# A hybrid four-branch mixer layer on one core: early merge-gate pairs, a first mLSTM chunk beside the last pairs, and block sums made operand by operand

## The chip, the core and the metric

The program runs on one core of one Trainium2 chip. Its time is device microseconds of one execution. Tile (a list scheduler with its own estimates of durations) turns the program text into one fixed instruction order per engine; priorities given in the text and the pools of tiles decide that order.

## What is computed

`x` is 2048 tokens by 1024 channels, float32. One layer, cut to what matters (in full it works chunkwise where that is said):

```python
def reference(x, norm_g, w_in, ..., w_branch, w_out, final_g):
    h = rmsnorm(x, norm_g)
    u = h @ w_in                               # 1024 -> 10256 columns
    (lru_x, lru_z, m_x, m_o, m_z, h_q, h_f, h_i, h_z,
     g_q, g_k, g_v, g_lr, g_z, merge) = split(u)
    y_a = rg_lru(causal_conv(lru_x)) * silu(lru_z)
    xm = silu(causal_conv(m_x))
    hm = sigmoid(m_o) * mlstm_chunkwise(q(xm), k(xm), v(m_x), log_i, log_f)
    y_b = (head_layernorm(hm) + m_skip * xm) * silu(m_z)
    y_c = head_rmsnorm(hgrn2(h_q, h_f, h_i)) * silu(h_z)
    y_d = head_rmsnorm(gla(g_q, g_k, g_v, g_lr)) * silu(g_z)
    proj = einsum('bsnw,nwd->bsnd', stack([y_a, y_b, y_c, y_d]), w_branch)
    merged = sum(sigmoid(merge) * proj, axis=2)
    return rmsnorm(x + merged @ w_out, final_g)
```

Every product is made to float32 accuracy from operands split in two parts: a high part (a copy rounded by ScalarE) and a low part (the difference), and three matmuls: high by high, high by low, low by high.

## The kernel before, in words

The tokens go through in two halves of 1024. In each half the stages follow one another in the program text, while the scheduler lets neighbours overlap.

*Input and first gates.* `load_first` (in half 0) loads and normalises the first 512 tokens and makes five merge gates from them; the result of each is taken from its bank by VectorE (line 353). Line 680 applies the norm to the other 512 tokens. `split_first` (line 305 ScalarE, line 306 VectorE or GpSimd) makes the operands a11 and a12 of the first tokens; x11, x12, x21, x22 are the four blocks of two token blocks by two channel blocks, four tiles each.

*Block sums.* `split_blocks` makes the other operands: a22 as it is, and the sums s1 to s4 (lines 375 to 378), each split again by lines 305 and 306. It goes tile by tile (k = 0 to 3), all operands of a tile before the next tile. The low parts of s1 and s2 are made by GpSimd, the rest by VectorE. The block x21 is kept in DRAM for later.

*Pairs.* `ahead_pairs` computes 33 pairs of column tiles per half. `ip_pair` computes one pair in Winograd's form: seven products of 12 matmuls (line 422, 128x512) with sums of weights (line 427) and of results (line 431) on VectorE; line 437 is ScalarE's copy of the first product out of its bank; the weight of each product is split by ScalarE (line 416) and GpSimd (line 417). Weights are loaded into three tiles `wr` and two tiles `gth`. The order of the pairs is a table, `GORD`: ('g', n) is n pairs of merge gates, ('z', n) n pairs of the paths that mixers use (mx, mo, mz, hq, hz, gz, gq, gk in this order), ('r', n) n pairs for the RG-LRU, ('d', n) the HGRN decays of number n, 'm' a step of the mLSTM's rows, and 't' sets an activation table. A gate pair leaves VectorE little after the sums. A pair of mx leaves a causal convolution (line 706, VectorE) and its silu (line 763). A pair of the RG-LRU has that convolution, the recurrence's gates (line 735, 24 matmuls of TensorE in the stretches counted below) and a scan. Results go to DRAM by SP's queue.

*Mixers.* `restore_block` loads x21 again. `mixers` interleaves the mLSTM's chunks (a generator `mlstm()`, eight chunks of 128 tokens a half, four heads each; `LEAD` = 8 of its steps are issued first) with tiles of HGRN2 and GLA and with merge-gate tiles that keep TensorE busy. In a chunk, lines 836 and 844 load xm and rows, line 855 computes the scores, lines 864, 871 and 880 values and transposes, line 892 and behind it transposes of the output gate and the rest. Line 227 (Ln) and line 1084 (Exp) are the root of a head's norm.

*Merge and output.* The branches' products and gates (line 268; the last gates' tanh, line 1301), then the output projection (line 280) and the final norm; rows leave by line 1358.

*Memory.* `Arena` holds NU = 16 units of 128 x 516 floats; pairs take their two result tiles from its first NG = 10 units and temporary tiles from the others. The first pairs' units for s1, s2 and s4 belong to tiles that in half 1 lie over the output rows of half 0.

In the trace's names, `wh`, `wl`, `hh`, `hl` and `s` are high and low parts (`s` of the sums), `mx` and `pb` are the eight banks that collect matmuls, `arena` is any unit, `ma` and `mb` tiles over the operands' places. `<-` stands between what is written and what is read.

Of the kernel before, what the change touches and what calls it, by code (L numbers as in the profile page):

```python
# [17 lines left out]
HT = 1024  # tokens of a half  # L18
DM = 1024
KT = 8  # k tiles of d_model  # L20
U = 516  # columns of one arena unit
NU = 16  # arena units that stay
NA = 4  # tiles of two units that are the arena's outside of the fast products
NY = 8  # the same, and branch outputs in the merge
NP = 6  # merge gates (of 32) computed between the mixers
NE = 5  # of these, so many for the first tokens while the others are split
EPS = 1e-6
NPB = 2  # PSUM banks of the input projection; the other ones are the mixers'
NG = 10  # arena units of the fast products; the other ones are what follows them
PRE = (("mx", 4), ("mo", 4), ("mz", 4), ("hq", 4), ("hz", 4), ("gz", 4), ("gq", 2), ("gk", 2))  # paths to DRAM, with their tiles  # L30
# [5 lines left out]
NW = 6  # L36
DG = (0,1)
# [4 lines left out]
GORD = [('r',1),('z',2),('r',1),('z',2),('r',1),('z',2),('r',1),('z',6),('g',8),('t',0),('m',0),('g',1),('m',0),('g',1),('m',0),('g',1),('m',0),('d',0),('m',0),('g',99),('d',1),('z',2)]  # L42
NORM = {"hz": "hnw", "gz": "gnw"}  # gate paths with the norm's weight in them
SILU = ("lz", "mz", "hq", "hz", "gz")
FILL = [0, 2, 0, 0, 0, 1, 0, 0, 1, 0, 0, 0, 2, 0]  # merge gates projected before each stage of the mixers

# columns of the packed per-channel vectors
# [10 lines left out]
# channel-major column tiles of the input projection, in the order of wc  # L58
# [10 lines left out]
# constants that depend on shapes alone  # L69
# [29 lines left out]
class Arena:  # L99
    """Units of U columns, handed out in program order, round and round; pairs start at even units."""  # L100
# [47 lines left out]
class Trunk:  # L148
    def __init__(self, ctx, tc, a, out, dbg=None):
# [8 lines left out]
        self.wr = [c.tile([P, 528], F32, name=f"wr{k}") for k in range(3)]  # L158
# [9 lines left out]
        self.mi = 0  # L168
        self.ydram = [self.dram.tile([4, P, HT], F32, name=f"y{n}") for n in range(4)]
# [34 lines left out]
    def bank(self):  # L204
        self.mi += 1
        return self.mx[self.mi % (8 - NPB)]

# [31 lines left out]
    def wpieces(self, aps):  # L239
        nc = self.nc  # L240
        r = []
        with self.prio(self.EV):
            for ap in aps:
                w = ap.shape[-1]
                i = self.wi
                self.wi += 1
                raw, hi, lo = self.wr[i % 3][:, :w], self.wh[i % NW][:, :w], self.wl[i % NW][:, :w]
                nc.sync.dma_start(raw, ap)
                nc.scalar.activation(hi, raw, AF.Copy)  # L249
                nc.gpsimd.tensor_tensor(lo, raw, hi, op=ALU.subtract)  # L250
                r.append((hi, lo))
# [4 lines left out]
    def proj_ch(self, pieces, rh, rl, sink, ns=(0, 1)):  # L256
        """128 columns of a product for 512 tokens at a time from weight pieces of 4 k tiles
        each: sink(token slice, PSUM [128, 512])."""
# [23 lines left out]
    def ip_tok(self, pieces, ncol, evac, single=8):  # L282
        """Token-major column group: evac(first chunk, PSUM [128 tokens, chunks, ncol]); chunks one by one from some."""
# [10 lines left out]
    def ip_tok_k(self, pieces, evac, ks):  # L294
        """The same for 256 columns, k outermost: the operands' tiles are done with one by one."""
# [13 lines left out]
    def split_first(self, xs):  # L309
        """The normalised input of the first tokens"""  # L310
# [7 lines left out]
    def load_first(self, xs):  # L318
        """The first tokens, and merge gates from them before the norm's factor is known"""
# [40 lines left out]
    def split_blocks(self, xs, st):  # L360
        """The other blocks (two of tokens by two of channels) that the products take: one more as it
        is, four sums; the block left out goes to DRAM."""
        nc = self.nc
        V, G = nc.vector, nc.gpsimd
        a, b = slice(0, 512), slice(512, 1024)

        def own(name, i, k):
# [3 lines left out]
        for k in range(4):  # L371
            x11, x21, x12, x22 = xs[k][:, a], xs[k][:, b], xs[4 + k][:, a], xs[4 + k][:, b]
            self.split("a22", self.hh[4 + k][:, b], self.hl[4 + k][:, b], x22, V)
            nc.sync.dma_start(self.adram[k], x21)
            V.tensor_tensor(x22, x21, x22, op=ALU.add)
            V.tensor_tensor(x21, x11, x21, op=ALU.subtract)
            V.tensor_tensor(x11, x22, x11, op=ALU.subtract)
            V.tensor_tensor(x12, x12, x11, op=ALU.subtract)
            self.split("s2", *own("s2", 0, k), x11, G)
            self.split("s3", self.hh[k][:, b], self.hl[k][:, b], x21, V)  # L380
            self.split("s1", *own("s1", 1, k), x22, G)
            self.split("s4", *own("s4", 2, k), x12, V)
        self.free(*xs)

    def restore_block(self):
        """The block left out of the products, where its sum was."""
# [13 lines left out]
    def ip_pair(self, t0, t1, fin):  # L400
# [57 lines left out]
    def ahead_pairs(self):  # L458
# [10 lines left out]
        def temp():  # L469
            return self.T(NG, NU)  # L470

# [1069 lines left out]
```

## Time and profile before

| | us |
|---|---|
| three runs | 2739.0, 2732.94, 2736.58 |
| median | 2736.58 |
| profiled execution, span | 2737.5 |
| TensorE busy | 2603.8 (95%) |
| GpSimd busy | 1499.7 (55%) |
| VectorE busy | 1736.1 (63%) |
| ScalarE busy | 1291.6 (47%) |

The profiled execution shows no time of its own beside its span, so the span is taken for it. Half 0's pairs run from about 52 to 760 us, its mixers to about 1200, its merge and output to about 1420; half 1 follows in the same order. The busy time of TensorE counts a matmul from its issue to a modelled end, with waits inside, so a stretch in which matmuls stand further apart can still look busy; how many matmuls a stretch holds says more.

### The profile page before, as it was taken

What the parts mean: (1) busy time and instruction counts of PE and PEld (TensorE: products, weight loads), DVE (VectorE), ACT (ScalarE), POOL (GpSimd) and SP (SyncE); (2) the same over time, 40 slices, a digit from 0 to 9 for tenths busy, and PEclk for the clock granted to TensorE, in tenths of its full rate; (3) what the DMA queues carried; (4) which work ended last, traced back from release to release, by engine and by line L of the source; (5) the groups of instructions that cost most, each with busy time, mean ns of one, the idle gap of its engine ahead of it and who ended that gap; (6) DMA issues with size and microseconds to landing.
All of it is one profiled execution on the core that took longest, in us unless ns stands there. A gap on an engine that the chain in (4) does not pass through costs nothing. (4 is left out here: it accounts for less than half of the span.)

```text
span 2737.5 us, 45829 instructions
## 1 busy us (share of the span) xinstructions
PE 2603.8 (95%) x16800; PEld 2153.6 (79%) x16800; DVE 1736.1 (63%) x2907; ACT 1291.6 (47%) x2763; POOL 1499.7 (55%) x1273
## 2 busy tenths in 40 slices
PE   7889999999989898999999999999999999999999
PEld 5667788877878876778977777888787888777789
DVE  8987853346667767743478878533477677776332
ACT  5554554334444565542465545533344445644433
POOL 5556644444546545567476666444455556554753
PEclk9999999999999999999999999999999999989999
DMA  6132334243454435795442322433335533458821
GB/s 227 61 109 89 101 119 139 98 145 103 148 170 128 121 121 189 253 317 165 155 138 94 110 91 89 139 116 108 135 113 179 167 118 106 146 190 308 273 93 74
DMA packets 227072, 393.03 MB, mean 144 GB/s; under 512 B 20720, under 2 KB 78080, under 8 KB 226848
## 3 DMA queue, kind: packets, MB, share of 16 engines
q1 hardware_dynamic: 226848, 390.11, 42.7%
q8 instruction: 132, 2.16, 0.3%
q14 instruction: 92, 0.75, 0.1%
HBM read 270.42 MB, written 119.60 MB: 142 GB/s over the span
## 5 line engine op out<-in xcount | busy, mean ns | idle before, releaser
L417 POOL TENSOR_TENSOR wl<-wr,wh 128x512 fp32r<-128x512 f32 x264 | 371.6, 1411 | 302.4 <-ACT wh L416 294.4
L417 POOL TENSOR_TENSOR wl<-gth,wh 128x512 fp32r<-128x512 f32 x198 | 284.4, 1437 | 294.6 <-ACT wh L416 284.2
L422 PE MATMUL mx<-s,wh 128*128 128x512 f32 x1296 | 408.5, 395 | 11.3 <-DVE s L306 4.7
L431 DVE TENSOR_TENSOR arena<-arena,mx 128x512 f32<-128x512 f32 x348 | 229.4, 681 | 221.8 <-PE mx L422 208.5
L250 POOL TENSOR_TENSOR wl<-wr,wh 128x512 fp32r<-128x512 f32 (+1 forms) x176 | 250.4, 1431 | 175.4 <-ACT wh L249 139.8
L422 PE MATMUL mx<-hh,wh 128*128 128x512 f32 x760 | 302.0, 397 | 11.9 <-DVE arena L431 10.2
L422 PE MATMUL mx<-hh,wl 128*128 128x512 f32 x760 | 302.3, 398 | 3.1 <-POOL wl L417 3.1
L422 PE MATMUL mx<-hl,wh 128*128 128x512 f32 x760 | 302.0, 397 | 2.0 <-DVE hl L306 2.0
L422 PEld LDWEIGHTS mx<-s,wh 128*128 128x128 f32 x1296 | 243.9, 188 | 70.6 <-DVE s L306 7.1
L268 PE MATMUL pb<-hh,wh 128*128 128x512 f32 x704 | 286.9, 409 | 7.4 <-ACT hh L1284 2.6
L268 PE MATMUL pb<-hl,wh 128*128 128x512 f32 x704 | 286.5, 407 | 5.8 <-DVE hl L1285 5.8
L268 PE MATMUL pb<-hh,wl 128*128 128x512 f32 x704 | 284.3, 404 | 0.0
L416 ACT ACTIVATE wh<-wr 128x512 fp32r<-128x512 f32 x264 | 164.5, 627 | 232.7 <-PE mx L422 98.4
L280 PE MATMUL pb<-wh,hh 128*128 128x256 f32 (+1 forms) x880 | 254.2, 290 | 3.7 <-ACT arena L1006 1.5
L422 PE MATMUL mx<-s,wl 128*128 128x512 f32 x648 | 256.2, 396 | 0.9 <-POOL wl L417 0.9
L280 PE MATMUL pb<-wl,hh 128*128 128x256 f32 (+1 forms) x880 | 253.4, 288 | 1.7 <-POOL wl L250 1.7
L280 PE MATMUL pb<-wh,hl 128*128 128x256 f32 (+1 forms) x880 | 253.5, 288 | 0.0
L416 ACT ACTIVATE wh<-gth 128x512 fp32r<-128x512 f32 x198 | 124.4, 629 | 246.6 <-DVE gth L427 201.6
L249 ACT ACTIVATE wh<-wr 128x512 fp32r<-128x512 f32 (+1 forms) x176 | 110.0, 629 | 161.9 <-PE pb L268 106.6
L422 PEld LDWEIGHTS mx<-hh,wh 128*128 128x128 f32 x760 | 144.3, 190 | 50.1 <-ACT arena L218 11.0
L422 PEld LDWEIGHTS mx<-hh,wl 128*128 128x128 f32 x760 | 143.6, 189 | 41.0 <-POOL wl L417 8.2
L422 PEld LDWEIGHTS mx<-hl,wh 128*128 128x128 f32 x760 | 144.0, 189 | 38.1 <-DVE hl L306 3.2
(614 smaller groups left out, 6177.6 us busy)
## 6 DMA issues: line engine op xcount, KB each, us to landing
wr<-in_wc_dram SPq DMA_DIRECT2D x246, 256.0 KB, 2.7
g<-arena SPq DMA_DIRECT2D x52, 512.0 KB, 3.4
gth<-in_wc_dram SPq DMA_DIRECT2D x66, 256.0 KB, 2.8
wr<-in_wb_dram SPq DMA_DIRECT2D x64, 256.0 KB, 3.0
hl<-y SPq DMA_DIRECT2D x32, 512.0 KB, 5.9
arena<-g SPq DMA_DIRECT2D x48, 256.0 KB, 3.9
arena<-in_xT_dram SPq DMA_DIRECT2D x32, 256.0 KB, 5.1
lw<-g SPq DMA_DIRECT2D x32, 256.0 KB, 3.4
```

Source lines behind the costliest of these rows:

```text
L249: nc.scalar.activation(hi, raw, AF.Copy)
L250: nc.gpsimd.tensor_tensor(lo, raw, hi, op=ALU.subtract)
L268: nc.tensor.matmul(ps, w[:, ws], h[:, ts], start=(k == 0 and i == 0), stop=(k == nk - 1 and i == 2))
L280: self.nc.tensor.matmul(v, h[:, cs], w[:, ws], start=(first and i == 0), stop=(last and i == 2))
L416: A.activation(hi, w, AF.Copy)
L417: G.tensor_tensor(lo, w, hi, op=ALU.subtract)
L422: nc.tensor.matmul(ps, wp[:, ws], xp, start=(k == 0 and i == 0), stop=(k == 3 and i == 2))
L431: V.tensor_tensor(o, x, y, op=ALU.add)
```

## The change

- `NU` grows from 16 to 22 units, `NV` = 16 keeps the pairs' temporary tiles to units 10 to 15. The memory comes from a smaller scratch of the kernel's dynamic DMA (`dynamic_dma_scratch_size=1024`). A fourth raw weight tile is added for the gate and output projections (`NR` = 4; the pairs still use three).
- `split_blocks` works operand by operand: s2 for all four tiles, then s1, s4, s3, a22; four more units hold the sum s2.
- In the first pair of a half the product with a12 comes second and waits in its bank until it is added.
- `GORD` starts with two gate pairs, and gate pairs stand between those of the RG-LRU and of mx.
- 'c' in `GORD` is one step of `mlstm()`: the loads and scores of the first chunk are issued before the last two path pairs, in units 16 to 21. The mixers then issue two steps less at their start.

```diff
-NU = 16
+NU = 22
+NV = 16
+NR = 4
-GORD = [('r',1),('z',2),('r',1),('z',2),('r',1),('z',2),('r',1),('z',6),('g',8),('t',0),('m',0),('g',1),('m',0),('g',1),('m',0),('g',1),('m',0),('d',0),('m',0),('g',99),('d',1),('z',2)]
+GORD = [('g',2),('r',1),('z',1),('g',1),('z',1),('r',1),('g',1),('z',2),('r',1),('g',1),('z',2),('r',1),('z',6),('g',3),('t',0),('m',0),('g',1),('m',0),('g',1),('m',0),('g',1),('m',0),('d',0),('m',0),('g',99),('d',1),('c',0),('z',1),('c',0),('z',1)]
...
     def bank(self):
+        if self.pairs:
+            return self.bank8()
...
-        for k in range(4):
-            x11, x21, x12, x22 = xs[k][:, a], xs[k][:, b], xs[4 + k][:, a], xs[4 + k][:, b]
-            self.split("a22", self.hh[4 + k][:, b], self.hl[4 + k][:, b], x22, V)
-            nc.sync.dma_start(self.adram[k], x21)
-            V.tensor_tensor(x22, x21, x22, op=ALU.add)
-            V.tensor_tensor(x21, x11, x21, op=ALU.subtract)
-            V.tensor_tensor(x11, x22, x11, op=ALU.subtract)
-            V.tensor_tensor(x12, x12, x11, op=ALU.subtract)
-            self.split("s2", *own("s2", 0, k), x11, G)
-            self.split("s3", self.hh[k][:, b], self.hl[k][:, b], x21, V)
-            self.split("s1", *own("s1", 1, k), x22, G)
-            self.split("s4", *own("s4", 2, k), x12, V)
+        ds = [self.T(0, NU) for k in K]
+        for k in K:
+            d = ds[k][:, :512]
+            nc.sync.dma_start(self.adram[k], x21[k])
+            V.tensor_tensor(x11[k], x11[k], x21[k], op=ALU.subtract)
+            V.tensor_tensor(d, x22[k], x11[k], op=ALU.subtract)
+            self.split("s2", *own(0, k), d, G)
+        for k in K:
+            V.tensor_tensor(x21[k], x21[k], x22[k], op=ALU.add)
+            self.split("s1", *own(1, k), x21[k], G)
+        for k in K:
+            V.tensor_tensor(x12[k], x12[k], ds[k][:, :512], op=ALU.subtract)
+            self.split("s4", *own(2, k), x12[k], V)
+        for k in K:
+            self.split("s3", self.hh[k][:, b], self.hl[k][:, b], x11[k], V)
+        for k in K:
+            self.split("a22", self.hh[4 + k][:, b], self.hl[4 + k][:, b], x22[k], V)
+        self.free(*ds)
...
-    def ip_pair(self, t0, t1, fin):
+    def ip_pair(self, t0, t1, fin, first=False):
...
         p = product("a11", b11)
         with self.prio(self.EV):
             A.activation(c11, p, AF.Copy)
+        if first:
+            q = product("a12", b21)
         wsum(b11, b12, b11)
         wsum(w2, b22, b11)
         p = product("s2", w2)
         add(c21, c11, p)
+        if first:
+            add(c11, c11, q)
...
-        p = product("a12", b21)
-        add(c11, c11, p)
+        if not first:
+            p = product("a12", b21)
+            add(c11, c11, p)
...
+            elif n == "c":
+                self.ar.base, self.ar.lim = NV, NU
+                with self.prio(RLAT):
+                    next(self.other)
+                self.ar.base, self.ar.lim = 0, None
...
-            for _ in range(LEAD):
+            for _ in range(LEAD - 2):
                 next(other, None)
...
-    nc = bacc.Bacc("TRN2", target_bir_lowering=False, num_devices=1)
+    nc = bacc.Bacc("TRN2", target_bir_lowering=False, num_devices=1, dynamic_dma_scratch_size=1024)
```

Line numbers of the changed file are larger: 306 becomes 311, 353 becomes 358, 375 and 376 (the sums of x22 with x21, and of x11 with x21) become 387 and 383, 417 becomes 432, 427 becomes 442, 227, 1084 and 1301 become 232, 1114 and 1331.

**VectorE, at the start of half 0's pairs.** Before, around the first block sums (`gth_95<-pb_98` is the fifth gate's result, the `mqk`, `gx` and `gv` copies belong to the setup):

```order
L680 SCALAR_TENSOR_TENSOR arena<-arena,pvt,xb_247 128x512 x8
L427 TENSOR_TENSOR wr_79<-wr_80,wr_79 128x512
L306 TENSOR_TENSOR hl_75<-arena,hh_67 128x512
L306 TENSOR_TENSOR hl_76<-arena,hh_68 128x512
L353 TENSOR_TENSOR gth_95<-pb_98,xa_235 128x512
...
L375 TENSOR_TENSOR arena<-arena 128x512 x3
L427 TENSOR_TENSOR gth_95<-wr_81,wr_79 128x512
L375 TENSOR_TENSOR arena<-arena 128x512
```

Now:

```order
L383 TENSOR_TENSOR arena<-arena 128x512 x4
L311 TENSOR_TENSOR hl_75<-arena,hh_67 128x512
L311 TENSOR_TENSOR hl_76<-arena,hh_68 128x512
L358 TENSOR_TENSOR gth_96<-pb_99,xa_236 128x512
...
L384 TENSOR_TENSOR arena<-arena 128x512 x4
L387 TENSOR_TENSOR arena<-arena 128x512 x4
L311 TENSOR_TENSOR hl_71<-arena,hh_63 128x512
L311 TENSOR_TENSOR hl_72<-arena,hh_64 128x512
L311 TENSOR_TENSOR hl_73<-arena,hh_65 128x512
L311 TENSOR_TENSOR hl_74<-arena,hh_66 128x512
L311 TENSOR_TENSOR hl_78<-arena,hh_70 128x512
```

The differences of x11 and x21 (L383) moved ahead of the fifth gate's result, and the last low part of a12 (`hl_78`) behind the sums of s2 and s1 and the low parts of s3.

**GpSimd, at the start of half 1's pairs.** Before:

```order
L417 TENSOR_TENSOR wl_93<-wr_79,wh_87 128x512
L417 TENSOR_TENSOR wl_90<-wr_81,wh_84 128x512
L417 TENSOR_TENSOR wl_89<-wr_79,wh_83 128x512
L417 TENSOR_TENSOR wl_91<-wr_80,wh_85 128x512
L306 TENSOR_TENSOR s_0_11366<-arena,s_0_11366 128x512
L306 TENSOR_TENSOR s_4_11370<-arena,s_4_11370 128x512
L306 TENSOR_TENSOR s_1_11367<-arena,s_1_11367 128x512
```

Now:

```order
L311 TENSOR_TENSOR s_0_11367<-arena,s_0_11367 128x512
L311 TENSOR_TENSOR s_1_11368<-arena,s_1_11368 128x512
...
L311 TENSOR_TENSOR s_6_11373<-arena,s_6_11373 128x512
L311 TENSOR_TENSOR s_7_11374<-arena,s_7_11374 128x512
L432 TENSOR_TENSOR wl_94<-wr_79,wh_88 128x512
L432 TENSOR_TENSOR wl_92<-wr_81,wh_86 128x512
L432 TENSOR_TENSOR wl_89<-gth_95,wh_83 128x512
```

The weights' low parts (`wl`) of the first pair stood ahead of the eight low parts of s1 and s2 and now stand behind them.

**ScalarE, near the end of half 0's mixers** (ACT_TABLE_LOAD brings in the tables of the function that follows). Before, the two loads behind the tanh of the gates:

```order
L1082 ACTIVATE arena,ssq_205<-mx_99 128x128 x4
L227 ACT_TABLE_LOAD
L227 ACTIVATE ssq_204<-ssq_204,small 128x4
L227 ACTIVATE ssq_205<-ssq_205,small 128x4
L1084 ACT_TABLE_LOAD
L1084 ACTIVATE ssq_204<-ssq_204 128x4
```

Now, from the first tanh on:

```order
L1331 ACT_TABLE_LOAD
L1331 ACTIVATE arena<-arena 128x512
L1112 ACTIVATE arena,ssq_205<-mx_105 128x128 x4
L232 ACT_TABLE_LOAD
L232 ACTIVATE ssq_205<-ssq_205,small 128x4
L1112 ACTIVATE arena,ssq_206<-mx_100 128x128
L1114 ACT_TABLE_LOAD
L1114 ACTIVATE ssq_205<-ssq_205 128x4
L1112 ACTIVATE arena,ssq_206<-mx_100 128x128 x3
L1120 ACTIVATE arena<-mx_105,ssq_205 128x128 x4
L232 ACT_TABLE_LOAD
L232 ACTIVATE ssq_206<-ssq_206,small 128x4
```

Four more head norms stand behind the first tanh than before, and loads between them; the whole program has 49 loads where it had 29.

## Rows read from the trace of the kernel before

**Rows 1.** The page, part 1: busy time, share of the span, instructions.

```profile
PE 2603.8 (95%) x16800; PEld 2153.6 (79%) x16800; DVE 1736.1 (63%) x2907; ACT 1291.6 (47%) x2763; POOL 1499.7 (55%) x1273
```

**Rows 2.** Windows: start:end, length; busy us (instructions) of PE, PEld, DVE, ACT, POOL; clock, DMA.

```profile
50.00:100.00 50.00, 35.95 (x136) 25.64 (x136) 49.46 (x76) 21.79 (x35) 30.76 (x20) 0.93 0.11 32
100.00:150.00 50.00, 46.41 (x187) 36.38 (x186) 45.92 (x57) 27.15 (x43) 31.91 (x21) 0.93 0.36 125
...
200.00:250.00 50.00, 49.60 (x215) 39.84 (x214) 30.87 (x40) 23.45 (x38) 28.37 (x23) 1.00 0.28 90
```

**Rows 3.** Windows of line 422 alone: TensorE's matmuls, its weight loads.

```profile
50.00:86.00 36.00, 23.66 (x84) 15.91 (x84) 0.95 0.12 37
86.00:200.00 114.00, 93.97 (x373) 73.46 (x373) 0.94 0.26 88
400.00:550.00 150.00, 150.00 (x649) 121.68 (x648) 1.00 0.35 116
1422.00:1440.00 18.00, 14.15 (x58) 10.59 (x59) 1.00 0.36 126
1440.00:1550.00 110.00, 91.60 (x373) 71.97 (x372) 0.95 0.24 82
```

**Rows 4.** Windows of line 735 alone, the RG-LRU's gate matmuls.

```profile
50.00:200.00 150.00, 6.96 (x24) 4.19 (x24) 0.94 0.23 76
1400.00:1550.00 150.00, 6.39 (x24) 4.35 (x24) 0.97 0.32 111
```

**Rows 5.** Timeline of TensorE: start, us, instruction [idle before <- what ended it].

```profile
63.77 0.69 PE L422 MATMUL mx<-s,wh 128*128 128x512 f32 x2 [3.45 <-DVE gv L625]
...
164.47 0.77 PE L422 MATMUL mx<-hh,wh 128*128 128x512 f32 x1 [5.09 <-DVE arena L431]
```

**Rows 6.** Timeline of VectorE in half 0's first pairs.

```profile
55.58 2.83 DVE L375 TENSOR_TENSOR arena<-arena 128x512 f32<-128x512 f32 x3
...
60.05 1.75 DVE L375 TENSOR_TENSOR arena<-arena 128x512 f32<-128x512 f32 x1
...
149.34 5.59 DVE L706 SCALAR_TENSOR_TENSOR arena<-arena,hmc 128x512 f32<-128x512 f32 x6
...
162.45 1.88 DVE L431 TENSOR_TENSOR arena<-arena,mx 128x512 f32<-128x512 f32 x3
```

**Rows 7.** Timeline of GpSimd in half 0, the first splits of sums.

```profile
57.95 4.97 POOL L306 TENSOR_TENSOR s<-arena,s 128x512 fp32r<-128x512 f32 x3 [1.29 <-ACT s L305]
```

**Rows 8.** Timelines of GpSimd and of ScalarE at the start of half 1's pairs.

```profile
1424.12 12.47 POOL L306 TENSOR_TENSOR s<-arena,s 128x512 fp32r<-128x512 f32 x8
...
1422.25 6.35 ACT L305 ACTIVATE s<-arena 128x512 fp32r<-128x512 f32 x12
```

**Rows 9.** Timeline of TensorE at the mixers' start, half 0 and half 1.

```profile
763.94 1.09 PE L880 MATMUL mx<-cst,ma 128*128 128x128 f32 x4 [6.48 <-DMA ma<-pxm]
...
788.90 1.40 PE L855 MATMUL mx<-ma,mqk 128*128 128x128 f32 x5 [3.66 <-DVE mmu L922]
...
2117.72 1.65 PE L855 MATMUL mx<-ma,mqk 128*128 128x128 f32 x6 [3.81 <-DMA ma<-pxm]
```

**Rows 10.** Line 836, a chunk's load: landing; then who waited, us, times.

```profile
DMA to landing us min/median/max: 2.7/3.1/8.1
...
  PE mx L855: 12.8, 9
```

**Rows 11.** Windows of the mixers, half 0 and half 1, as in rows 2.

```profile
756.00:1200.00 444.00, 405.15 (x4206) 346.96 (x4205) 306.04 (x678) 222.17 (x645) 228.73 (x240) 0.95 0.54 175
2112.00:2560.00 448.00, 418.84 (x4275) 359.89 (x4274) 311.27 (x684) 228.01 (x659) 240.44 (x249) 0.95 0.55 181
```

**Rows 12.** Timeline of ScalarE around a table load, and the window it lies in.

```profile
1196.83 1.28 ACT L227 ACT_TABLE_LOAD   x1
1198.12 0.48 ACT L227 ACTIVATE ssq<-ssq,small 128x4 f32<-128x4 f32 x2
...
1180.00:1200.00 20.00, 20.00 (x119) 15.52 (x118) 4.80 (x10) 10.10 (x29) 5.25 (x5) 1.00 0.91 307
```

More of the change, by code (lines that the diff above doesn't have):

```diff
@@ L157, in __init__ @@
         self.hl = [c.tile([P, HT], F32R, name=f"hl{k}") for k in range(KT)]
-        self.wr = [c.tile([P, 528], F32, name=f"wr{k}") for k in range(3)]
+        self.wr = [c.tile([P, 528], F32, name=f"wr{k}") for k in range(NR)]
         self.wh = [c.tile([P, 528], F32R, name=f"wh{k}") for k in range(NW)]
@@ L168, in __init__ @@
         self.mi = 0
+        self.pairs = False
         self.ydram = [self.dram.tile([4, P, HT], F32, name=f"y{n}") for n in range(4)]
@@ L246, in wpieces @@
                 self.wi += 1
-                raw, hi, lo = self.wr[i % 3][:, :w], self.wh[i % NW][:, :w], self.wl[i % NW][:, :w]
+                raw, hi, lo = self.wr[i % NR][:, :w], self.wh[i % NW][:, :w], self.wl[i % NW][:, :w]
                 nc.sync.dma_start(raw, ap)
@@ L365, in split_blocks, with own @@
         a, b = slice(0, 512), slice(512, 1024)
-        def own(name, i, k):
+        K = range(4)
+        def own(i, k):
             t = st[4 * i + k]
             return t[:, 0:512], t[:, U:U + 512]
-        for k in range(4):
-            x11, x21, x12, x22 = xs[k][:, a], xs[k][:, b], xs[4 + k][:, a], xs[4 + k][:, b]
-            self.split("a22", self.hh[4 + k][:, b], self.hl[4 + k][:, b], x22, V)
-            nc.sync.dma_start(self.adram[k], x21)
-            V.tensor_tensor(x22, x21, x22, op=ALU.add)
-            V.tensor_tensor(x21, x11, x21, op=ALU.subtract)
-            V.tensor_tensor(x11, x22, x11, op=ALU.subtract)
-            V.tensor_tensor(x12, x12, x11, op=ALU.subtract)
-            self.split("s2", *own("s2", 0, k), x11, G)
-            self.split("s3", self.hh[k][:, b], self.hl[k][:, b], x21, V)
-            self.split("s1", *own("s1", 1, k), x22, G)
-            self.split("s4", *own("s4", 2, k), x12, V)
+        x11, x21 = [xs[k][:, a] for k in K], [xs[k][:, b] for k in K]
+        x12, x22 = [xs[4 + k][:, a] for k in K], [xs[4 + k][:, b] for k in K]
+        ds = [self.T(0, NU) for k in K]
[16 more added lines that the diff above has]
+        self.free(*ds)
         self.free(*xs)
@@ L405, in ip_pair @@
         with self.prio(self.EV):
-            b11, b12, b22 = (r[:, :512] for r in self.wr)
+            b11, b12, b22 = (r[:, :512] for r in self.wr[:3])
             b21, w2 = self.gth
@@ L469, in temp @@
         def temp():
-            return self.T(NG, NU)
+            return self.T(NG, NV)
         def silu2(n, x):
@@ L531, in ahead_pairs @@
         rows = (i for h in range(2) for i in self.mlstm_rows(h, temp))
+        self.other = self.mlstm()
+        self.pairs = True
+        first = True
         for n, i in GORD:
@@ L537, in ahead_pairs @@
                     next(rows, None)
-            if n in "tm":
+            elif n == "c":
[3 more added lines that the diff above has]
+                self.ar.base, self.ar.lim = 0, None
+            if n in "tmc":
                 continue
             for tiles, fin in ({"g": g, "z": z, "r": r}[n][:i] if n != "d" else [decays([2 * i, 2 * i + 1])]):
-                self.ip_pair(*tiles, fin)
+                self.ip_pair(*tiles, fin, first)
+                first = False
             if n != "d":
@@ L544, in ahead_pairs @@
         assert not g and not z and not r and next(rows, 1)
+        self.pairs = False
     def setup(self):
@@ L1185, in mixers @@
         self.gates_ahead(next(fill))
-        other = self.mlstm()
+        other = self.other
         due = 0.0
```

## The prediction

> **What bounds the kernel.** The engine table comes first: TensorE is busy for 95% of the span [rows 1], so time can only be won where its matmuls stand apart. The windows of the first pairs show such a place. From 50 to 150 us TensorE is busy for 35.95 and 46.41 of each 50 us, VectorE for 49.46 and 45.92. From 200 to 250 us VectorE falls to 30.87 and TensorE rises to 49.60 [rows 2]. VectorE limits the early pairs, and nothing after them.
>
> Waiting matmuls count as busy, so I count matmuls instead. From 400 to 550 us nothing waits: 649 of line 422 in 150 us, 0.2311 us each [rows 3]; a product of 12 takes 2.77 us, a pair of 84 takes 19.4. Half 0 from 50 to 86 us has 84 of them [rows 3], worth 19.4 of 36 us. From 86 to 200 us there are 373, and 24 of the RG-LRU's own [rows 3, 4]: 397 x 0.2311 = 91.7 of 114 us, so 22.3 lost. Half 1, whose pairs begin at about 1422 us, has 58 by 1440 [rows 3], worth 13.4 of 18; then 373 and 24 by 1550 [rows 3, 4], worth 91.7 of 110, so 18.3 lost. (A few records may be missing from a trace, which makes these losses upper bounds.)
>
> The timelines tell why. TensorE waits 3.45 us at 63.77 for operands, and 5.09 us at 164.47 for an addition of line 431 [rows 5]. Before that addition VectorE ran convolutions of line 706, six in 5.59 us from 149.34 on; the three additions came at 162.45, behind more of them [rows 6]. An addition sets a bank free, so TensorE stops when several additions stand behind convolutions.
>
> **The change part by part. Order of the pairs.** A pair costs VectorE eleven sums of 1.88/3 = 0.63 us [rows 6], 7 us, whatever its kind; a gate pair has little more. A pair of mx adds twelve taps of 5.59/6 = 0.93 us [rows 6] and four more operations, by the same rates 22 in all; a pair of r adds six taps, eight operations and two scans, at the tap's rate 22 too. TensorE takes 19.4. Before, r, mx, mx, r stand first: 4 x 2.6, over 10 us of backlog, on top of the splits' own. Now it is g, g, r, mx, g, mx, r, g: a gate pair gives over 10 us back ahead of every second debtor, so 2 x 2.6, some 5 us, are owed at most. The two output tiles and the banks let TensorE run a product or two, 3 to 6 us, ahead. So I keep 5 of the 22.3 us in half 0, **17.3 won**, and 4 of the 18.3 in half 1, **14.3 won**. Bounds: nothing, if a backlog of 5 us still stops the banks; all of both.
>
> **Operand by operand, half 0.** The differences of x11 and x21 now stand ahead of the fifth gate's result (the block of VectorE's rows shown): four of 2.83/3 = 0.94 us [rows 6], so the first pair starts some 3.5 us later than before. Then a11 and most of a12 run, 22 matmuls; the last split of a12 (hl_78) stands behind eight sums and four splits. Beside GpSimd's splits one operation of VectorE took 1.75 us at 60.05, without them 0.94 [rows 6, 7]. The block of eight is 8 x 4.97/3 = 13.3 us of GpSimd [rows 7]. With eight of VectorE's thirteen operations at 1.75 and five at 0.63, from 57 on, hl_78 is ready at 74; with all at 0.94, at 69. From then on little waits: by 86 us 22 + 12/0.2311 = 74 matmuls, or 95, against 84. I take 78, since three operations of 1.75 stand in the row for three splits: **1.4 lost**, between 2.3 lost and 2.5 won. With the order: 16, between 2 lost and 25.
>
> **Operand by operand, half 1.** On GpSimd the eight splits now stand ahead of the first pair's weights; before, four weights came first. They take 12.47 us, ScalarE's twelve copies 6.35 from 1422.25 on [rows 8], and cannot start sooner, since four of the tiles lie where the last output rows leave. So TensorE has no weight before 1428.6 and starts near 1430, at first at the lower clock: some 35 matmuls by 1440 against 58 [rows 3], 23 x 0.2311 = **5.3 lost**. With the 14.3 this is 9 won, between 0 and 16.
>
> **First chunk beside the last pairs.** The chunk's scores move about 229 matmuls ahead of the pairs' end, into 22 - 16 = 6 units of their own. Its matmuls and its work on ScalarE and VectorE are not less; late pairs leave VectorE free [rows 2]. Its loads join SP's queue behind writes of the same data; each holds the queue for a landing, 3.1 us by the median [rows 10], while the next pair's weights are asked for four products, 11 us, ahead. With that cover gone, each would cost 3. What vanishes: TensorE's waits at the mixers' start, 6.48 and 3.66 us in half 0, 3.81 in half 1 [rows 9], 13.95 in all. Late next is the first chunk's output gate (the transposes of line 892 come first there in the changed order), whose load waits for the last pair's units and lands, 3.1 [rows 10], then the second chunk's, an estimate of 1.4 more: 9 for two halves. **5 won**, between 0 and 9.
>
> **Head norms among tanh.** With one chunk less behind the border, the merge's first tanh (line 1301) stands ahead of six head norms per half instead of two. Ln, Exp and Tanh alternate, and ScalarE loads a table 49 times where it did 29 times, all twenty more at the two ends of the mixers. One takes 1.28 us [rows 12]: 25.7 us of ScalarE. Before, such loads fell into 20 us in which TensorE was busy throughout and ScalarE half the time [rows 12]. That nearest row says nothing lost; as TensorE's order is fixed and each load holds a head's result, I charge **3 us**, between 0 and 25.7.
>
> In the row no idle time stands around a load: it ends at 1198.11, the next instruction begins at 1198.12 [rows 12]. The Trainium skill (ScalarE: Activation LUTs, What ACT_TABLE_LOAD costs) adds a drain of 1380 ns to each of 1283 ns, 2.66 us per switch, and its section on table sets wants calls batched by set, which speaks against this change. By that page twenty switches hold ScalarE for 53 us instead of 25.7. The row disagrees on the drain, and I go by the row.
>
> **The rest.** The first product keeps its bank of eight until a12 is added: nothing, or one product, 2.8, if banks run short. A fourth raw weight buffer and the wider arena let loads start sooner in the mixers, where TensorE idles for 444 - 405.15 = 39 and 448 - 418.84 = 29 us [rows 11]; I take nothing, between 14 lost and 14 won. The smaller scratch serves no queue used here.
>
> **The sum.** 2737.5 - 16 - 9 - 5 + 3 = 2710.5. The profiled execution is 0.9 us above the median of the runs, 2736.58, so the time is **2710**.
>
> **Rivals.** *More than that:* arena and fourth buffer also take a third of the mixers' 68 us of idle time [rows 11], 23 less: 2687. For it: the mixers wait for loads [rows 9, 10]. Against: most units were there already.
>
> *The loss only moves:* VectorE's work is the same, so the convolutions meet later pairs. Then the order's 31.6 are not won: about 2741 (2737.5 + 1.4 + 5.3 - 5 + 3 - 0.9). For it: VectorE has 5 of 100 us to spare [rows 2]. Against: from 200 us on it has 19 of 50 [rows 2].
>
> *The first pairs wait longer:* blocks of splits on two engines that hinder each other delay TensorE by another 4 us in half 0 and 6 in half 1: 2720. For it: the 1.75 us [rows 6]. Against: the operands were made in one go before as well.
>
> *Tables on the path:* every load delays TensorE by its 1.28 us [rows 12]; 22.7 more than charged, 2732. For it: heads at the end of a half have few others beside them. Against: merge products fill TensorE there [rows 12]. (With the page's 2.66 us it would be 2760.)
>
> *Slower:* the mLSTM's chunk loads are issued sooner into the wider arena, among the other mixers' on one queue, and land later. TensorE already waits for them, 12.8 us over nine waits; the longest landing is 8.1 against 3.1 [rows 10]. If each of sixteen chunks is later by 3 us of those 5, that is 48: 2758. It decides from 27/16 = 1.7 us per chunk on. Against: a chunk less behind the border leaves more time per load.
>
> **Chances.** As forecast 0.58, more 0.13, longer first pairs 0.08, the loss moves 0.10, tables 0.06, slower 0.05. A measurement of this kernel tells 0.2%, 5.5 us, from no change. The first three are faster by more than that, and parts of the next two: 0.84. Of those two 0.10 is no change and 0.01 slower, with the last case 0.06. The range reaches down past the second case to 2682, and up to 2731, past longer first pairs and nearly to the tables.
>
> **What would show it.** Right: 440 or more of the pairs' matmuls from 86 to 200 us and no wait over 3 us for an addition there; TensorE idle for some 8 us after 1422; waits of 4 to 5 us at the border, the transposes' first; table loads at the mixers' ends without gaps of TensorE behind them. Wrong: pairs after 200 us that lose what the early ones win, gaps of over 1 us behind table loads, or idle time in the mixers above 39 and 29 us.

## The result, and the profile after

The changed kernel takes 2800.8 us (median of 4 runs, 2799.45 to 2809.91) against 2737.79 for the one before (4 runs, 2732.94 to 2743.06): a ratio of 1.0243, 95% interval 1.0221 to 1.0265. It is 63 us slower where 27 us faster was forecast. The rest of this text takes the 63 us apart.

The page's first parts, of the kernel after:

```profile
span 2799.9 us, 45661 instructions
...
PE 2628.1 (94%) x16800; PEld 2174.8 (78%) x16800; DVE 1740.9 (62%) x2907; ACT 1312.4 (47%) x2783; POOL 1514.5 (54%) x1273
```

The same matmuls are there as in [rows 1]. VectorE has the same work within 5 us, and ScalarE has 20 more instructions (the table loads).

The windows of line 437, which answer to [rows 3], show the early pairs:

```profile
50.00:86.00 36.00, 17.34 (x53) 12.58 (x54) 0.76 0.18 63
86.00:200.00 114.00, 105.79 (x445) 84.09 (x444) 0.99 0.30 100
400.00:550.00 150.00, 150.00 (x649) 121.46 (x648) 1.00 0.37 127
...
1454.00:1472.00 18.00, 14.09 (x52) 10.94 (x53) 0.91 0.28 88
1472.00:1582.00 110.00, 103.17 (x434) 82.14 (x434) 0.98 0.30 101
```

From 86 to 200 us 445 matmuls stand where 373 stood, and in the like stretch of half 1 434 for 373. That part of the forecast came true. But up to 86 us there are 53 for 84, and half 1's pairs begin at 1454 us, not 1422. The mixers, in the windows that answer to [rows 11]:

```profile
756.00:1200.00 444.00, 392.34 (x4089) 337.26 (x4090) 304.19 (x660) 221.11 (x623) 223.09 (x236) 0.91 0.50 160
...
2141.00:2594.00 453.00, 402.29 (x4125) 343.38 (x4125) 304.29 (x661) 225.48 (x637) 226.43 (x239) 0.91 0.50 164
```

TensorE idles for 51.7 and 50.7 us instead of 39 and 29, and the granted clock is 0.91 instead of 0.95. So a good part of the loss sits where the diff hardly edits a line.

To see it for every kernel, I divide each half of a trace at the starts of three matmuls: the pairs' first and last, and the last output matmul of HGRN2 and GLA (line 1072 before). Durations in us; "start" is the first matmul of half 0's pairs, "border" runs from the mixers' end to the first matmul of half 1's pairs, "end" to the end of the last matmul:

| kernel | start | pairs 0 | mixers 0 | border | pairs 1 | mixers 1 | end |
|---|---|---|---|---|---|---|---|
| before | 52.0 | 703.3 | 439.9 | 227.2 | 689.4 | 429.1 | 190.5 |
| after | 62.1 | 692.6 | 450.3 | 249.5 | 686.0 | 453.7 | 199.5 |
| e4, order alone | 52.1 | 692.6 | 440.1 | 223.3 | 680.2 | 432.6 | 191.5 |
| e9, pairs only | 55.8 | 694.6 | 435.8 | 244.3 | 682.0 | 437.0 | 188.5 |
| e10, and buffer | 62.3 | 688.7 | 436.7 | 241.5 | 681.7 | 445.8 | 190.0 |
| e5, and chunk | 61.6 | 692.5 | 458.5 | 232.3 | 680.4 | 458.9 | 177.2 |
| e6, after, tanh late | 62.8 | 692.9 | 442.6 | 248.3 | 685.9 | 446.4 | 198.3 |
| e3, wide arena alone | 51.2 | 703.0 | 459.0 | 236.8 | 690.1 | 465.0 | 193.7 |
| e11, arena unused | 52.1 | 703.1 | 434.8 | 227.0 | 689.9 | 430.9 | 190.5 |
| e12, other rate | 51.7 | 703.2 | 452.3 | 221.5 | 690.3 | 435.6 | 188.5 |
| e13, sums in half 0 only | 56.8 | 695.0 | 435.7 | 231.0 | 679.7 | 443.1 | 188.5 |

### The profile page after: what moved, and what is told of

It is laid out like the page before. It is cut to its first block, busy times and chain, and to the rows that moved or that the text cites. A ratio compares the mean times of both kernels' runs of the same rounds, so it can differ in the third digit from the quotient of the medians.

```text
span 2799.9 us, 45661 instructions
## 1 busy us (share of the span) xinstructions
PE 2628.1 (94%) x16800; PEld 2174.8 (78%) x16800; DVE 1740.9 (62%) x2907; ACT 1312.4 (47%) x2783; POOL 1514.5 (54%) x1273
## 4 chain that ended last, share of the span: by engine, by line
PE 67%; DVE 13%; DMA 7%; ACT 4%; POOL 4%; issue 4%; SPq 0%; POOLq 0%; ACTq 0%; DVEq 0%
PE mx L437 33%; PE pb L273 13%; PE pb L437 9%; PE pb L285 5%; DMA arena<-rdram 2%; POOL wl L432 1%; PE mx L285 1%; DVE arena L736 1%; DMA y<-arena 1%; PE mx L1102 1%; PE mx L1101 1%; DMA ob<-in_x_dram 1%; DVE mb L1038 1%; PE pb L809 1%; PE mx L1015 1%
## 5 line engine op out<-in xcount | busy, mean ns | idle before, releaser
L446 DVE TENSOR_TENSOR arena<-arena,mx 128x512 f32<-128x512 f32 x386 | 252.9, 681 | 185.5 <-PE mx L437 166.4
L437 PE MATMUL mx<-hh,wl 128*128 128x512 f32 x808 | 320.8, 397 | 9.3 <-POOL wl L432 9.3
L437 PE MATMUL mx<-hh,wh 128*128 128x512 f32 x808 | 319.4, 396 | 5.3 <-ACT wh L431 5.3
L437 PE MATMUL mx<-hl,wh 128*128 128x512 f32 x808 | 319.2, 395 | 0.0
L273 PE MATMUL pb<-hh,wh 128*128 128x512 f32 x704 | 292.9, 418 | 20.1 <-DVE ma L1376 6.2
L437 PEld LDWEIGHTS mx<-s,wh 128*128 128x128 f32 x1296 | 244.2, 188 | 62.8 <-POOL s L311 6.3
L273 PE MATMUL pb<-hh,wl 128*128 128x512 f32 x704 | 290.2, 412 | 0.0
L437 PEld LDWEIGHTS mx<-hh,wl 128*128 128x128 f32 x808 | 152.0, 188 | 50.8 <-POOL wl L432 16.0
L437 PEld LDWEIGHTS mx<-hh,wh 128*128 128x128 f32 x808 | 152.3, 189 | 44.3 <-ACT wh L431 6.6
L273 PEld LDWEIGHTS pb<-hh,wh 128*128 128x128 f32 x704 | 140.3, 200 | 54.1 <-issue 7.5
```

Source lines behind the costliest of these rows:

```text
L273: nc.tensor.matmul(ps, w[:, ws], h[:, ts], start=(k == 0 and i == 0), stop=(k == nk - 1 and i == 2))
L437: nc.tensor.matmul(ps, wp[:, ws], xp, start=(k == 0 and i == 0), stop=(k == 3 and i == 2))
L446: V.tensor_tensor(o, x, y, op=ALU.add)
```

## The experiments

**One part at a time: e1 to e4.** e1 takes the chunk out of the changed kernel, e2 the fourth buffer. e3 and e4 add to the kernel before the arena alone and the order alone.

```diff
e1
-('d',1),('c',0),('z',1),('c',0),('z',1)]
+('d',1),('z',2)]
-            for _ in range(LEAD - 2):
+            for _ in range(LEAD):
e2
-NR = 4
+NR = 3
e3
-NU = 16
+NU = 22
+NV = 16
-            return self.T(NG, NU)
+            return self.T(NG, NV)
-bacc.Bacc("TRN2", target_bir_lowering=False, num_devices=1)
+bacc.Bacc("TRN2", target_bir_lowering=False, num_devices=1, dynamic_dma_scratch_size=1024)
e4
-GORD = [('r',1),('z',2),('r',1),...
+GORD = [('g',2),('r',1),('z',1),('g',1),('z',1),('r',1),...,('d',1),('z',2)]
```

> The changed kernel with the mLSTM's first chunk back behind the last pairs (no 'c' steps, LEAD of 8 steps again); all else stays. Theory 1, the chunk beside the last pairs disturbs the mixers: most of the 66 us lost from the mixers to the next half goes away, 2725 to 2745. Theory 2 (fourth raw weight buffer) and theory 3 (wider arena): the mixers stay as slow, 2785 to 2815. Theory 4, every edit reshuffles the mixers' fixed order and none is the cause: the loss changes by 10 us or more either way, 2750 to 2800, with the number of table loads (41 here, 29 before, 49 after).

Measured: 2802.82 us, 1.0241 (1.0168 to 1.0314). Theory 1 alone is out: without the chunk the mixers stay as slow (461.7 and 463.7 us).

> The changed kernel with three raw weight buffers instead of four. Theory 2, weight loads issued sooner hold SP's queue ahead of the mixers' loads: 2730 to 2750, and the wait of GpSimd's weight splits for ScalarE's copies falls from 104 us towards 65 in half 0. Theories 1 and 3: unchanged within 10 us, 2790 to 2810. Theory 4: somewhere from 2770 to 2810 (47 table loads).

Measured: 2798.24 us, 1.0224 (1.0157 to 1.0292). Theory 2 is out.

> The kernel before with the wider arena alone (22 units, pairs' temporary tiles kept to 10 to 15, smaller DMA scratch). Theory 3, the mixers take more tiles at once and their fixed order gets worse: slower by 30 to 60 us, 2770 to 2800. Theories 1 and 2: 2730 to 2745. Theory 4: between, with 41 table loads.

Measured: 2811.18 us, 1.0272 (1.0217 to 1.0326). The arena by itself, in the kernel before, costs as much as the whole change (73 us for 63, with intervals that overlap), and more than the theory's 30 to 60. The pairs keep their time; the mixers take 19 and 36 us longer.

> The kernel before with the new order of the pairs alone, without the chunk's steps. By the forecast the early pairs win 17 and 14 us and the mixers are left alone: 2705 to 2715. If the loss only moves: 2735 to 2740. Theory 4: the mixers change by 10 us or more though nothing in them was edited; 31 table loads.

Measured: 2713.41 us (4 runs), 0.9917 (0.9897 to 0.9936). The order alone wins 25 us, and the mixers stay where they were. This version beats both kernels. The windows of line 422 in e4, from 86 us and from the 18th us of half 1's pairs:

```profile
86.00:200.00 114.00, 105.87 (x444) 83.94 (x443) 0.98 0.33 109
...
1426.00:1536.00 110.00, 104.00 (x434) 83.08 (x433) 0.97 0.30 103
```

They hold 444 and 434 matmuls, as many as the kernel after: what it gains in the early pairs is the order's. The count flatters the win in half 0. Line 735, the RG-LRU's gate matmuls, has only 12 matmuls in e4 up to 200 us where it had 24 [rows 4]; the others stand later:

```profile
50.00:200.00 150.00, 2.93 (x12) 2.25 (x12) 0.97 0.28 92
```

**Units, tables, dose: e5 to e8.** e5 bars units 16 to 21 in the arena's `get` from the mixers on until the next half's sums. e6 puts a dependency without a semaphore of its own between the last head norm's Exp and each tanh of the merge. e7 is e3 with units 18 to 21 barred. e8 is e3 with `low = NV + 2 * NA`.

```diff
e5, e7 (e7 with 18 <= v)
-                  if u + k <= hi and (k == 1 or u % 2 == 0) and not any(self.used[u:u + k])]
+                  if u + k <= hi and (k == 1 or u % 2 == 0) and not any(self.used[u:u + k])
+                  and not (self.hold and any(16 <= v < 22 for v in range(u, u + k)))]
...
+                self.ar.hold = False
                 self.split_blocks(x, st)
...
+            self.ar.hold = True
             self.restore_block()
e6
-                        A.activation(t[:, :512], t[:, :512], AF.Tanh, scale=0.5)
+                        self.after(A.activation(t[:, :512], t[:, :512], AF.Tanh, scale=0.5), self.norm)
```

> The changed kernel, whose six new units are barred from the mixers, the merge and the output (the pairs and the first chunk keep them). If the units that the mixers get are the cause of the loss, the mixers return to 440 and 430 us and the early pairs keep their gain: 2695 to 2715, with 29 table loads. If the first chunk or the fourth buffer hurts as well, 2720 or more.

Measured: 2772.33 us, 1.0134 (1.0096 to 1.0172). The first expectation missed, the second holds: barring the units gives back 28 us and leaves 34, though only 29 tables are loaded. The mixers stay slow (458.5 and 458.9), so something besides the units acts on them.

> The changed kernel, wide arena and all, in which every tanh of the merge comes behind the last head norm of its half on ScalarE: 25 table loads instead of 49. If the alternating tables (25.7 us of ScalarE, the gaps behind the heads' norms) make the loss, 2735 to 2755. If the freer use of units makes it in other ways, 2775 to 2800.

Measured: 2780.9 us, 1.0161 (1.0121 to 1.0201): 20 us less than the kernel after (10 to 35 by the two intervals), which is nearly the forecast's upper bound for the loads (25.7), but far from the whole loss.

> The kernel before with the wide arena, of which mixers, merge and output may use two of the six new units (49 table loads). If the loss grows with the units, a third of 73 us, 2755 to 2770; if any other number of units upsets an order that was tuned for sixteen, 2780 or more or, by luck, 2740.

Measured: 2792.57 us, 1.0204 (1.0168 to 1.0239). Two units cost three quarters of what six cost; the loss does not follow their number.

> The kernel before with the wide arena, but with the limit that the last tiles of the mixers get left at 24 units instead of 30 (57 table loads). If the late limit, which keeps units free for the merge, were the cause, 2735 to 2750; if the units in the middle of the mixers are, 2790 to 2820.

Measured: 2794.18 us, 1.021 (1.0174 to 1.0245). The late limit is not the main cause: with it as it was, 56 of the 73 us stay.

**Is it the order of the mixers' rows: e9 to e12.** I compared VectorE's rows from the mixers to the output, trace with trace, by program text and shape, and took the share in matching stretches. They stand as before to 90 and 100% (half 0, half 1) in e4, to 31 and 36% in the kernel after, 45 and 38% in e3, 54 and 54% in e5, 39 and 35% in e12. The share shows where the order changed; it does not measure the price. e9 is e5 without the chunk and with three buffers; e10 is e9 with four; e11 is e3 with all six units barred; e12 is the kernel before with one number changed.

```diff
e9 (on e5; e10 without the first two lines)
-NR = 4
+NR = 3
-('d',1),('c',0),('z',1),('c',0),('z',1)]
+('d',1),('z',2)]
-            for _ in range(LEAD - 2):
+            for _ in range(LEAD):
e11 (on e3)
+                  and not (self.hold and any(16 <= v < 22 for v in range(u, u + k)))]
e12
-RATE = 0.65
+RATE = 0.6
```

> The change's work on the pairs alone: the new order, the operand by operand sums and the early a12, with the new units barred from the mixers, merge and output, three raw weight buffers, and the first chunk behind the pairs. The instructions' order in the mixers is then nearly that of before (93 to 98% of the rows of three engines). If that order is what the mixers' time hangs on, they take 440 and 430 us: 2695 to 2715. If the sums made operand by operand cost the pairs more than the order wins, 2720 or more.

Measured: 2745.56 us (10 runs), 1.0037 (1.0021 to 1.0053). Mixers as expected, yet 32 us slower than e4: the second half of the sentence holds. The table puts most of it at the border (244.3 for 223.3). Besides the sums, the step from e4 to e9 holds the early a12, the units for the sums and the eight banks by turns for the pairs' other matmuls; no run parts these.

> The kernel of e9 with the fourth raw weight buffer. If the buffer hurts by itself, 2725 or more; if it helps the mixers' gates, 5 to 10 us faster than e9; if only the chunk made e5 slow, within 10 us of e9 (87 to 96% of the mixers' rows stand as before).

Measured: 2748.05 us (8 runs), 1.0054 (1.0036 to 1.0073). The buffer neither helps nor hurts measurably, so the 24 us from e10 to e5 (15 by the profiled spans) are the chunk's in this order of steps: 22 and 13 in the mixers, 9 and 13 given back behind them. With the arena open to the mixers, taking the chunk out won nothing (e1).

> The kernel before with the wide arena and the smaller scratch, all six new units barred from mixers, merge and output: the order of VectorE and ScalarE is row for row that of before. If memory as such (addresses, the scratch) costs anything, 2745 or more; if only the order of instructions does, 2732 to 2743.

Measured: 2737.86 us, 1.0012 (0.9996 to 1.0029). The memory as such costs nothing that can be measured.

> The kernel before with one number changed: the mLSTM's steps come in at 0.60 of the other mixers' steps, not 0.65. Neither arena, buffer nor chunk is touched, but the mixers' rows fall into another order (35 to 57% as before). If any other order of the same work costs the mixers 18 to 36 us a half, 2770 to 2810; if arena and chunk cost by what they are, 2730 to 2750.

Measured: 2757.19 us, 1.0095 (1.0057 to 1.0132). Between the two: another order that has nothing to do with arena or chunk costs 21 us, less than expected for "any other order" and more than for none.

**Border and tables: e13 to e15.** In e13 half 1 makes its sums tile by tile, with a12 sixth, as before; it is e9 otherwise. e14 and e15 are e4 and e3 with the edit shown for e6.

```diff
e13
+        if half:
+            for k in range(4):
...
+            return
...
-        first = True
+        first = not self.half
```

> The kernel of e9 with the operand by operand sums and the early a12 in half 0 alone; half 1 makes its sums tile by tile as before. If the border of the halves pays for the sums, the merge of half 0 falls back from 244 to about 225 us: 2718 to 2728, and what is left over e4 is half 0's own price, 4 to 8 us. If the sums cost everywhere, 2735 to 2745.

Measured: 2736.75 us (10 runs), 1.0005 (0.9988 to 1.0021). The first forecast missed: the border falls from 244.3 to 231.0, the time by 9 us only. By the profiled spans e13 is 17.5 us over e4 (by the medians 23): 7 in half 0's start and pairs, 8 at the border, 10.5 in the mixers of half 1, whose rows again stand a little otherwise, and 8 given back elsewhere. Of the last three it stays open how they hang together.

> The kernel of e4 (order of the pairs alone) with every tanh of the merge behind the last head norm of its half: 25 table loads instead of 31. In that order only three loads a half stand at the mixers' end, 3.8 us of ScalarE: within 5 us of e4, 2708 to 2718. If a later tanh delays the merge's gates, 2720 or more.

Measured: 2716.4 us, 0.9938 (0.9915 to 0.9961): no change from e4, as expected.

> The kernel of e3 (wide arena alone) with every tanh of the merge behind the last head norm of its half: 25 table loads instead of 41. If the tables make most of the arena's 73 us, 2745 to 2765; if they make what they made in e6, 20 us or less, 2790 to 2805, and the rest is the order of the mixers' other rows.

Measured: 2803.85 us, 1.0266 (1.0237 to 1.0296): the same as e3 within the intervals, 7 us less by the medians. That is no proof that loads cost less in e3's order: 16 loads fewer at the price of e6 (20 us for 24) would be 13 us, and the two intervals leave some 17 us either way.

## Why the prediction was wrong, and where it was right

The steps, by the medians from one kernel to the next: order of the pairs 25 us won (before to e4), sums operand by operand 32 lost (e4 to e9), fourth buffer 2.5 lost, not measurable (e9 to e10), first chunk 24 lost (e10 to e5), arena open to the mixers 28 lost (e5 to after). This is one path; parts of it don't add up in every sequence (the arena alone costs 73 in the kernel before, and the chunk costs nothing where the arena is open, e1).

**The order of the pairs: right mechanism, a size somewhat too high.** The forecast was 31.6 won in both halves; measured 25, of which the pairs' own stages hold 10.7 and 9.2. The waits for additions are what went. TensorE's waits from 86 to 200 us, the longest group before and in e4 (total, times, longest):

```profile
PE mx L422 <- DVE arena L431: 6.8, 2, 5.1
...
PE mx L422 <- POOL wl L417: 2.3, 2, 1.7
```

With lines 422 and 735 counted together, 456 matmuls in half 0 leave 8.6 of the 114 us lost, where 5 were to be left. The loss did not move to later pairs: of the 50 matmuls (11.6 us) that e4 is ahead at 250 us, 10.6 us are left at the pairs' end.

**Operand by operand: the term was mis-sized in both halves.** I let the splits on GpSimd slow VectorE, by its 1.75 us [rows 6], with eight splits in 13.3 us and hl_78 ready at 74. In e9, which has these sums without the fourth buffer and the chunk, it came out so. GpSimd, VectorE and TensorE in e9, and the window of its pairs' matmuls:

```profile
59.65 13.45 POOL L313 TENSOR_TENSOR s<-arena,s 128x512 fp32r<-128x512 f32 x8
...
57.85 5.75 DVE L386 TENSOR_TENSOR arena<-arena 128x512 f32<-128x512 f32 x4
63.53 6.76 DVE L389 TENSOR_TENSOR arena<-arena 128x512 f32<-128x512 f32 x4
...
72.02 0.80 PE L439 MATMUL mx<-hl,wh 128*128 128x512 f32 x1 [9.66 <-DVE hl L313]
...
50.00:86.00 36.00, 18.29 (x54) 12.87 (x55) 0.67 0.11 37
```

What the sum had wrong is TensorE. Only 13 of the pairs' matmuls stood ahead of that wait, not 22. And behind its waits (6.29 us before the first pair, 9.66 here) the granted clock was at the lower of its two levels, 1.2 GHz, for some 5 us each time, with matmuls 0.43 us apart instead of 0.23: 0.67 in the mean from 50 to 86 us, 0.91 in e4. By 86 us 54 matmuls stand, where I took 78 and e4 has 81.

In the kernel after the two engines changed parts. The timelines of TensorE, VectorE and GpSimd at the start, and line 311 on GpSimd (shortest, median and longest in ns):

```profile
62.07 0.79 PE L437 MATMUL pb<-hh,wh 128*128 128x512 f32 x1 [4.80 <-DVE gth L358]
...
81.38 0.79 PE L437 MATMUL mx<-s,wh 128*128 128x512 f32 x1 [5.08 <-POOL s L311]
...
63.48 2.49 DVE L384 TENSOR_TENSOR arena<-arena 128x512 f32<-128x512 f32 x4
...
65.88 2.49 DVE L387 TENSOR_TENSOR arena<-arena 128x512 f32<-128x512 f32 x4
...
64.90 19.80 POOL L311 TENSOR_TENSOR s<-arena,s 128x512 fp32r<-128x512 f32 x7 [6.45 <-ACT s L310]
...
L311 POOL TENSOR_TENSOR s<-arena,s x8: 1264/1718/10626, 64.9 to 84.7; 128x512 fp32r<-128x512 f32 x8
```

VectorE's sums ran at 0.62 us each, and GpSimd's first split stood 10.63 us beside fifteen such operations of VectorE in one run; the other seven took 1.26 to 1.74 us, near the 1.66 of [rows 7]. The block that I had at 13.3 us lasted over 20, and TensorE waited 5.08 us at 81.38 for it. By 86 us 31 matmuls were missing, 7.2 us, about as many as in e9. The start came 10 us later than before: 4 of these are in e9 as well (I had 3.5), the other 6 come with the fourth buffer (62.3 in e10) and hardly change the count by 86 us (51 in e10). The Trainium skill (SBUF — State Buffer, Who interferes with whom) says that a VectorE instruction with two SBUF inputs contends with a GpSimd instruction that reads SBUF, and that issue order decides which of them blocks. The traces agree that one of the two stands still. Why it was VectorE in e9 and GpSimd here they don't show, since in both GpSimd's operation came into a run of VectorE's that had begun. Either way half 0 paid: e9's pairs end 5.7 us later than e4's, where I had 1.4.

In half 1 the price of 5.3 us overlooked who is queued behind the sums on VectorE. The border after, VectorE and TensorE (line 1376 takes the last output rows from their banks):

```profile
1422.00 1.29 DVE L311 TENSOR_TENSOR hl<-arena,hh 128x512 fp32r<-128x512 f32 x2
1423.20 0.42 DVE L1376 SCALAR_TENSOR_TENSOR ma<-pb,ma 128x256 f32<-128x256 f32 x1
...
1423.77 0.76 PE L273 MATMUL pb<-hh,wh 128*128 128x512 f32 x1 [6.20 <-DVE ma L1376]
```

And in e4, where sums and evacuations alternate:

```profile
1377.34 0.68 DVE L306 TENSOR_TENSOR hl<-arena,hh 128x512 fp32r<-128x512 f32 x1
1377.94 0.41 DVE L1346 SCALAR_TENSOR_TENSOR ma<-pb,ma 128x256 f32<-128x256 f32 x1
...
1378.50 0.47 PE L268 MATMUL pb<-hh,wh 128*128 128x512 f32 x1 [0.55 <-DVE ma L1346]
```

TensorE needs the banks for the next gates and stands 6.20 us instead of 0.55, because VectorE's unbroken run of sums comes first. e13 shows the price: with half 1's sums tile by tile, the stretch from the last output matmul to half 1's pairs falls from 39.2 us (e9) to 30.3, which is e4's value too, and the time by 9. With half 0's 5.7 that is 15 of the 32. The rest is only placed: 12 us lie in half 0's merge, before the sums begin (205.0 us in e9 and 193.0 in e4 from the mixers' end to the last output matmul).

**The first chunk: the border was right, the mixers were not looked at.** TensorE's waits there, in the kernel after:

```profile
756.15 0.63 PE L922 MATMUL mx<-cst,ma 128*128 128x128 f32 x4 [1.13 <-DMA ma<-pmo]
758.41 0.58 PE L285 MATMUL pb<-wh,hh 128*128 128x256 f32 x1 [1.64 <-DVE arena L446]
...
2142.36 0.63 PE L922 MATMUL mx<-cst,ma 128*128 128x128 f32 x4 [1.49 <-DMA ma<-pmo]
...
2144.37 0.55 PE L285 MATMUL pb<-wh,hh 128*128 128x256 f32 x1 [1.38 <-DVE arena L446]
```

In all 5.6 us stand for 13.95 [rows 9], so 8 us of these waits went where I wrote 5, and the transposes of the output gate come first, as forecast. (Only 36 matmuls a half, lines 885 to 931, moved ahead of the pairs' last, not the 229 that I named; no term hangs on them.) The step that failed is that I put the mixers behind the border at nothing: the chunk's work is "not less", I wrote, and did not ask in what order it falls. From e10 to e5 the chunk cost 24 us; TensorE's idle time in the mixers rose from 34.0 and 33.4 to 38.8 and 39.9 us, and a wait of 6.23 us stands behind half 0's. Where the rest lies stays open.

The longest gap of the kernel after goes with the open arena. Timelines of TensorE, VectorE and SP's queue in half 0, with the same place in half 1:

```profile
941.66 1.16 PE L885 MATMUL mx<-arena,mqk 128*128 128x128 f32 x8 [0.28 <-DMA arena<-pxm]
...
945.35 1.16 PE L901 MATMUL mx<-arena 128*128 128x128 f32 x8 [0.81 <-ACT arena L887]
...
948.13 0.39 PE L931 MATMUL mx<-Cst,arena 128*128 128x129 f32 x2
957.33 1.40 PE L1015 MATMUL mx<-mb 128*32 128x32 f32 x64 [8.82 <-DVE mb L1038]
...
2343.88 1.33 PE L1015 MATMUL mx<-mb 128*32 128x32 f32 x64 [9.45 <-DVE mb L1038]
...
943.00 1.14 DVE L904 SCALAR_TENSOR_TENSOR arena<-arena,mcols,cst 128x128 f32<-128x128 f32 x4 [6.11 <-DMA arena<-rdram]
...
925.61 5.92 SPq L253 DMA_DIRECT2D wr<-in_wc_dram  x4
...
939.01 0.37 SPq L874 DMA_DIRECT2D arena<-rdram  x1
```

VectorE stood for 6.11 us for a chunk's row, asked for at 939.01, behind the gate weights (5.92 us of SP's queue) and other transfers. It then worked until 957 with no pause of a microsecond, and TensorE waited 8.82 us with no gate product to run. The same place costs 9.45 us in half 1. The trace shows these links; no run removed one of them alone. Without the chunk but with the open arena, line 1015 waits there as well, 5.23 and 3.01 us in e1; with the chunk but the units barred (e5) no wait of half 0's mixers is longer than 3.38 us.

**Arena: "I take nothing, between 14 lost and 14 won" was the step that failed most.** I saw only what more units could allow, not that they decide the order on every engine. e11 (the old order with the wide arena's memory: no change), e3, e7 and e8 (other orders by more units: 54 to 73 us) and e12 (another order by a rate: 21) show that the mixers' time hangs on which units they may take and, in e12, on the order of their rows alone; the order before was a favourable one. That the arena costs by the order too is the plain reading, since unused units cost nothing; no run held the order and changed the units. In e3's mixers TensorE idles for 53.5 and 50.6 us, in e11's for 37.5 and 31.8, and the granted clock is 0.93 for 0.96 and 0.95. Why an arena's order is worse than a rate's is not settled.

**Tables: wrong cause, and the charge of 3 us was too small here.** It is mostly not the chunk that brings tanh ahead: e1, without it, still loads 41 tables, e3 41, and with the units barred e5 loads 29. That the merge's gate tiles get a free unit earlier would explain it, but is not shown. The gaps, ScalarE and TensorE after:

```profile
1129.06 1.28 ACT L232 ACT_TABLE_LOAD   x1
1130.36 0.30 ACT L232 ACTIVATE ssq<-ssq,small 128x4 f32<-128x4 f32 x1
1130.67 1.28 ACT L1036 ACT_TABLE_LOAD   x1
...
1132.72 1.14 ACT L1120 ACTIVATE arena<-mx,ssq 128x128 f32<-128x128 f32 x4
...
1133.14 1.25 PE L1124 MATMUL mx<-cst,arena 128*128 128x128 f32 x4 [2.29 <-ACT arena L1120]
...
1173.34 0.99 PE L1124 MATMUL mx<-cst,arena 128*128 128x128 f32 x3 [3.32 <-ACT arena L1120]
```

Two loads sit between a head's sum of squares and its scaling, and TensorE waits 2.29 and 3.32 us for it: the sign given ahead as proof against the step. No drain follows a load here either (1130.34 to 1130.36), so the 2.66 us of the Trainium skill (ScalarE: Activation LUTs, What ACT_TABLE_LOAD costs) were rightly set aside. Batching by set, as the Trainium skill's section on table sets (ScalarE: Activation LUTs, Table sets: the hidden batching unit) has it, was worth 20 us in the kernel after (e6); in e3 (e15) the runs cannot tell its price from nothing. These 20 us lie inside the arena's 28, since the loads rise from 29 to 49 at that step: e6 is 9 us slower than e5.

**The rivals.** The slower one that I named, late chunk loads, is not it. The landing of line 866 in the kernel after:

```profile
DMA to landing us min/median/max: 2.7/3.3/7.1
```

Before it was 3.1 and 8.1 [rows 10]; TensorE waits 5.8 us in all for these loads, and waited 21.6. No rival of mine let the order of the mixers' rows itself cost time, and so the range ended 70 us too low.

## What to carry to other kernels

When a scheduler fixes the order of every engine from the program and its pools, a wider pool or a step moved between stages is an edit of every stage that uses them: compare the rows of the stages that the change is not meant to touch, and leave them a wide range where they differ. Take the parts that leave those rows alone (here the order of the pairs, 2713 us) and bar new memory from stages that don't need it. A long run of independent work on one engine has a price in what is queued behind it: look for evacuations first.

## What the runs showed of the hardware

A split of 128x512 on GpSimd stood 10.63 us beside fifteen two-input operations of VectorE in one run, which kept 0.6 us each (after). In e9 the same eight splits took 1.71 us each by the median, and it was VectorE's sums that took up to 1.78 us instead of 0.67. Behind TensorE's waits of 6.29 and 9.66 us in e9, matmuls of 128x512 stood 0.43 us apart at the granted clock's lower level, 0.23 us at the upper one. A table load takes the same 1.28 us in the rows shown before and after, with no pause behind it; 24 loads fewer were worth 20 us in the kernel after.
